# Decoder trunk on one core: where layer 1's output projection starts feed-forward's loads, and who halves one of its weight blocks

## The chip, the core and the metric

The kernel runs on one core of a Trainium2 chip. The metric is the time of one execution in microseconds of the device; the median of three runs before the change is 1432.92 us (1432.63 to 1433.38). All points of time below are microseconds from the first instruction of one profiled execution.

## The reference, cut to what matters

Two layers, each a mixer block and a feed-forward block on 512 tokens of width 1024:

```python
x  = x + g1 * (merged @ w_out)                      # output projection
h2 = rmsnorm(x, norm2_w) * (1 + sc2) + sh2          # second norm
x  = x + g2 * ((silu(h2 @ w_gate) * (h2 @ w_up)) @ w_down)
```

`g1`, `g2`, `sc2`, `sh2` come from `c` through a matrix `w_ada`; everything is float32, with features on the 128 partitions and tokens along the free dimension.

## The kernel before

**A product.** TensorE gets float32 accuracy from three passes (`mm3`, L176): weight-high by data-high, weight-high by data-low, weight-low by data-high. So each weight block of 8 x 128 columns (512 KB) is fetched into a `raw` tile and halved into a `whi` and a `wlo` tile. There are two ways of halving. `split_w` (L515 and L518): ScalarE copies the high half, VectorE subtracts it from `raw`. `split_by_transfer` (L539, L540, L542): ScalarE writes high and minus high, and a transfer issued by POOL adds the block from memory once more onto `wlo`. The pools are small: three `raw` tiles (`RAW = 3`), five `whi`, five `wlo`, six `w` tiles for sums of blocks, 46 `big` tiles.

**Queues.** Fetches leave from SP's queue, transfers that accumulate from POOL's queue; each queue is worked in order, and an issue that waits for its tile holds everything behind it. During layer 1's output projection `in_order[0]` is set: there `sent` pins the transfers of a queue to the order of the program text. VectorE's halvings (L518) are pinned among each other as well; the other instructions of VectorE and ScalarE are placed by a planner that reorders them by its own estimate of when they are ready.

**Layer 1's output projection** (`tail`, L1576, with `middle=out_pairs`, L1646). Of the eight output column blocks, 0 and 1 are plain. Blocks 2 to 5 are the *quad*: two pairs computed with a seven-product scheme from seven weight loads, called S0 to S6 here (`Out.load`, L384). Its products come in this order, each for both pairs (z = 0, 1), each group four `mm3` of 256 columns: B11, B21, R1, -V, B22, T3, T4. S0 and S1 serve B11 and B21, S2 and S3 serve R1 and -V, S4 and S5 serve B22 and T3, S6 alone serves T4. After each group VectorE adds the result to `x` (`put`, L1649); T4 of a pair goes into the same accumulator that T3's `put` has just read. Then `tail` does blocks 6 and 7 (called C6 and C7) in two halves of 256 tokens; in the middle of block 6's second half TensorE sums the squares for the second norm of the first 256 tokens (`lead`, `stat`, the `pair<-big,ones` products). Then come feed-forward's first rows.

**Loads around it.** `next_w` loads up to five blocks ahead. The list after S6 is C6, C7, then R0 to R3 (feed-forward's first rows: gate and up, two blocks of k each, two fetches of 256 KB), then the first `GateUp` pair. That pair needs for each of gate and up a *raw block* (512 KB, `Sums.fetch`), two `w` tiles with fetches from SP and accumulating transfers from POOL (`Sums.begin`, L286, 2 x 256 KB each way), and two additions by VectorE (`Sums.add`, L321 and L322). `opening` (L547) starts gate's part from inside `out_pairs`: "fetch" begins the sums and fetches the raw block, "add" does the two additions. Up's sums are begun by `load_w` when R0 is loaded. Gate's raw block keeps its `raw` tile until the first pair is computed, much later.

**S6** (`Out.load`, sub 6) is halved like this: raw fetched from SP (L393), high and minus high by ScalarE (L394, L395), two accumulating transfers of 256 KB from POOL (L397).

**The dots.** Sixteen dot products with `w_ada` (`ada_halves`, two 128x512 instructions each, L672) give `g1` and `g2` of layer 1. `timed_dots` places them by a list of ticks (`DOT_TICKS`, one tick is 2048 output columns of TensorE); each dot's two fetches of 256 KB into `big` tiles (L668) are placed three ticks before it. Ticks 32 and 33 lie in the attention stage, ticks 46 to 52 in the last gates before the output projection.

Of the kernel before, what the change touches and what calls it, by code (L numbers as in the profile page):

```python
# [13 lines left out]
F32R = mybir.dt.float32r  # L14
BF16 = mybir.dt.bfloat16
I32 = mybir.dt.int32
AF = mybir.ActivationFunctionType
ALU = mybir.AluOpType
# [3 lines left out]
P = 128  # L22
# [19 lines left out]
C_BLOCKS = 8  # L42
# [32 lines left out]

DELAY = 3

DOT_TICKS = (6, 7, 18, 19, 21, 32, 33, 37, 40, 42, 44, 45, 46, 47, 48, 49)

TWO_PI = 2.0 * math.pi  # L80
RED1 = 6.28125
# [16 lines left out]
def hybrid_trunk(ctx, tc, xT, ws, ada, cols, pool_w, qk_w, crow, pos, con, out):  # L98
    nc = tc.nc
    V, A, T = nc.vector, nc.scalar, nc.tensor  # L100
# [3 lines left out]
    wp = ctx.enter_context(tc.tile_pool(name="wp", bufs=4))  # L104
# [6 lines left out]
    def nm(s):  # L111
        uid[0] += 1
        return f"{s}{uid[0]}"

    def bigt(dt=F32R):
        return big.tile([P, S], dt, tag="big", name=nm("big"))
# [4 lines left out]
    def ps_mm():  # L121
        return psum.tile([P, S], F32, tag="mm", name=nm("mm"), bufs=4)

    def ps_pair():
        return psum.tile([P, 2, S], F32, tag="pair", name=nm("pair"), bufs=2)
# [4 lines left out]
    def sm(shape, dt=F32, tag="sm", bufs=8):  # L130
        return small.tile(shape, dt, tag=tag, name=nm(tag), bufs=bufs)

    f32 = lambda ap: ap.bitcast(F32)
# [44 lines left out]
    def pin(ins):  # L178
        return tc.keep_in_program_order(ins)
# [83 lines left out]
    in_order = [False]  # L263

    def sent(ins):
        return pin(ins) if in_order[0] else ins
# [5 lines left out]
    HK = KT // 2  # L272
# [3 lines left out]
    class Sums:  # L276
# [12 lines left out]
        raw = None  # L289
# [38 lines left out]
    class GateUp:  # L328
# [10 lines left out]
        def load(self, sub):  # L339
            if sub < 2:  # L340
                return self.pair[sub].first(self.adding and sub == 0)
            if sub < 6:
                return self.pair[sub % 2].sums(sub // 2 - 1)
            raw = rawt()
            blocks = self.pair[0].blocks(1, 1) + self.pair[1].blocks(1, 1)
            fetch(raw, self.l, blocks)
            return split_w(raw, len(blocks))
# [32 lines left out]
    class Out(GateUp):  # L380
# [3 lines left out]
        def load(self, sub):  # L384
            if sub < 2:
                s = self.pair[sub]
                s.fetch()
                return split_by_transfer(s.raw, self.l, s.column(0))
            if sub < 6:
                return self.pair[sub % 2].sums(sub // 2 - 1)  # L390
            raw, hi, lo = rawt(), *[wp.tile([P, C_BLOCKS, P], F32R, tag=t, name=nm(t), bufs=5) for t in ("whi", "wlo")]
            for z, s in enumerate(self.pair):
                sent(nc.sync.dma_start(raw[:, z * HK:(z + 1) * HK], s.source(1, 1)))  # L393
            A.activation(hi, raw, AF.Copy)  # L394
            A.activation(lo, f32(hi), AF.Copy, scale=-1.0)  # L395
            for z, s in enumerate(self.pair):
                sent(nc.gpsimd.dma_start(lo[:, z * HK:(z + 1) * HK], s.source(1, 1), accum_op=ALU.add))  # L397
            return hi, lo

    class KeyValue:  # L400
        SUBS = 14
# [107 lines left out]
    def rawt():  # L509
        return wp.tile([P, C_BLOCKS, P], F32, tag="raw", name=nm("raw"), bufs=RAW)  # L510

    def split_w(raw, n):
        hi = wp.tile([P, C_BLOCKS, P], F32R, tag="whi", name=nm("whi"), bufs=5)
        with tc.issue_after(hold_hi[0].ins) if hold_hi[0] is not None else nullcontext():
            A.activation(hi[:, :n], raw[:, :n], AF.Copy)  # L515
        lo = wp.tile([P, C_BLOCKS, P], F32R, tag="wlo", name=nm("wlo"), bufs=5)
        with tc.issue_after(hold[0].ins) if hold[0] is not None else nullcontext():
            ins = V.tensor_sub(lo[:, :n], raw[:, :n], f32(hi)[:, :n])  # L518
        pin(ins)
        return hi, lo  # L520
# [13 lines left out]
    def split_by_transfer(raw, l, blocks):  # L534
        n = len(blocks)
        hi = wp.tile([P, C_BLOCKS, P], F32R, tag="whi", name=nm("whi"), bufs=5)
        lo = wp.tile([P, C_BLOCKS, P], F32R, tag="wlo", name=nm("wlo"), bufs=5)
        with tc.issue_after(last_gate[0].ins) if last_gate[0] is not None else nullcontext():
            A.activation(hi[:, :n], raw[:, :n], AF.Copy)  # L539
            A.activation(lo[:, :n], f32(hi)[:, :n], AF.Copy, scale=-1.0)  # L540
        for i, m, src in runs(l, blocks):
            sent(nc.gpsimd.dma_start(lo[:, i:i + m].rearrange("p b n -> p (b n)"), src, accum_op=ALU.add))  # L542
        return hi, lo
# [2 lines left out]

    def opening(z, what):  # L547
        sums = next(s for s, _ in list(items)[at[0]:] if type(s) is GateUp)
        if what == "fetch":
            for s in sums.pair[:1] if in_order[0] else sums.pair:  # L550
                s.begin()
            sums.pair[z].fetch()
        else:
            sums.pair[z].add()
# [7 lines left out]
    def load_w():  # L562
        while at[1] < min(at[0] + 1 + SUMS_AHEAD, len(items)):
            sums, sub = items[at[1]]
            if sums is not None and sub == 0:
                sums.begin()
            at[1] += 1
        sums, what = items[at[0]]
        at[0] += 1
        if sums is not None:  # L570
            return sums.load(what)
        l, blocks = what
        if raws:
            raw = raws.popleft()
        else:
            raw = rawt()
            fetch(raw, l, blocks)
        if by_transfer(l, blocks):
            return split_by_transfer(raw, l, blocks)
        with tc.issue_after(split_after[0].ins) if split_after[0] is not None else nullcontext():  # L580
            halves = split_w(raw, len(blocks))
        if (l, blocks[0]) == (0, ("in", 0, 3)):
            rotary()
        return halves
# [29 lines left out]
    def next_w(ahead=None):  # L614
        ahead = ahead_now[0] if ahead is None else ahead
        while at[0] < len(items) and len(loaded) <= ahead:
            loaded.append(load_w())
        return loaded.popleft()
# [59 lines left out]
    def timed_dots(l):  # L678
# [3 lines left out]
        def load(i):  # L682
            fetched[i] = ada_halves(l, BESIDE[l][i // KT], i % KT, False)

        for i, at_tick in enumerate(DOT_TICKS):
            events.append((at_tick - DELAY, 0, lambda i=i: load(i)))
# [419 lines left out]
    sums = scratch[:, 0].rearrange("p (t n) -> p t n", n=P)  # L1106
# [36 lines left out]
    y, t, r = [sm([P, TT], tag="rst", bufs=3) for _ in range(3)]  # L1143
# [22 lines left out]
    for l in range(L):  # L1166
# [7 lines left out]
        for n, (k, lo, hi) in enumerate([(k, 0, S) for k in range(KT)] if l == 0 else HALVES + REST):  # L1174
# [19 lines left out]
            w = held[k]  # L1194
# [191 lines left out]
        for j in range(2):  # L1386
# [12 lines left out]
            z = bigt(F32)  # L1399
# [133 lines left out]
        for step, j in GATE2:  # L1533
# [13 lines left out]
            t = sg2.pop(j)  # L1547
# [97 lines left out]
        def out_pairs():  # L1645

            def put(n, src, c):
                by = (minus if n % 2 else mod[l][:, G1])[:, n:n + 1]
                return V.scalar_tensor_tensor(x[n][:, c], src, by, x[n][:, c], op0=ALU.mult, op1=ALU.add)  # L1649

            both, fm = range(2), out_forms
            n1, n2_ = OUT_FIRST, [n + 1 for n in OUT_FIRST]
            a, c = [None] * 2, [None] * 2
            w = [next_w() for _ in both]
            for z in both:
                a[z] = ps_mm()[:, :BLOCK]
                group(a[z], w[z], 0, "B11", True, fm, True)
                put(n1[z], a[z], early)
            e = ps_pair()
            for z in both:  # L1660
                group(e[:, z, :BLOCK], w[z], 1, "B21", True, fm, True)
            for z in both:
                ins = put(n1[z], e[:, z, :BLOCK], early)
            with tc.issue_after(ins.ins):
                for i in range(HK):
                    out_form_two(i)
            w = [next_w() for _ in both]
            for z in both:
                c[z] = ps_mm()[:, :BLOCK]
                group(c[z], w[z], 0, "R1", True, fm)  # L1670
                put(n2_[z], c[z], late)
            for z in both:
                group(a[z], w[z], 1, "-V", False, fm)
                put(n1[z], a[z], late)
            opening(0, "fetch")
            w = [next_w() for _ in both]
            for z in both:
                group(c[z], w[z], 0, "B22", False, fm)
                put(n1[z], c[z], late)
                n2.add(n1[z], 0, S)  # L1680
            for z in both:
                group(a[z], w[z], 1, "T3", False, fm)
                put(n2_[z], a[z], late)
            opening(0, "add")
            w = next_w()
            for z in both:
                group(a[z], w, z, "T4", False, fm)
                put(n2_[z], a[z], early)
                n2.add(n2_[z], 0, S)

        ahead_now[0] = 4
        if l == 0:
# [359 lines left out]
```

## Time and profile before

| | us |
|---|---|
| median of three runs | 1432.92 |
| the profiled execution, whole | 1433.26 |
| its span, first to last instruction | 1431.5 |
| TensorE busy in the span | 1420.0 |
| VectorE busy | 1102.9 |
| ScalarE busy | 779.7 |
| POOL busy | 146.6 |

The span is 1.76 us shorter than the profiled execution, which is 0.34 us above the median. TensorE's own loads of weights overlap its products. In the rows, PE is TensorE, DVE is VectorE, ACT is ScalarE, SPq is SP's queue; `mm` and `pair` are accumulators, `x` the residual stream, `in_ws` the weights in memory.

### The profile page before, as it was taken

How to read it: one execution, taken by the hardware profiler on the slowest of the kernel's cores; microseconds unless marked ns; L12 is line 12 of the kernel's file. 1: busy time of each engine (PE TensorE's matmuls, PEld its weight loads, DVE VectorE, ACT ScalarE, POOL GpSimd, SP SyncE). 2: the span in 40 equal slices, each digit the busy share in tenths (PEclk: the TensorE clock that was granted, in tenths of full speed). 3: DMA queues.
4: the chain of work that ended last, by engine and by line, in shares of the span. 5: the costliest groups of instructions: out<-in, count | busy, mean ns of one | idle time of the engine just before them, and what ended most of it. 6: DMA issues, size and time to landing. Idle time of an engine off the chain costs nothing.

```text
span 1431.5 us, 23124 instructions
## 1 busy us (share of the span) xinstructions
PE 1420.0 (99%) x8600; PEld 1265.8 (88%) x8600; DVE 1102.9 (77%) x2097; ACT 779.7 (54%) x1317; POOL 146.6 (10%) x181
## 2 busy tenths in 40 slices
PE   9999999999999999999999999999999999999998
PEld 8888888888998998999988888878888989989998
DVE  8989888768897867776799986766878847657676
ACT  6667667633762542545455775665557625435452
POOL 0111001101010201010002001010210101000110
PEclk9999999999999999999999999999999999999999
DMA  9757788867366767655447566678964637636452
GB/s 384 229 141 208 207 218 209 234 203 222 92 164 209 208 171 208 185 164 181 168 161 215 172 172 160 161 190 219 255 147 111 175 112 185 171 107 185 135 129 82
DMA packets 114449, 259.35 MB, mean 181 GB/s; under 512 B 13208, under 2 KB 33824, under 8 KB 114336
## 3 DMA queue, kind: packets, MB, share of 16 engines
q1 hardware_dynamic: 87616, 198.22, 40.6%
q0 software_dynamic: 26128, 59.52, 23.6%
q8 instruction: 67, 1.10, 0.3%
q14 instruction: 46, 0.38, 0.1%
q10 hardware_dynamic: 592, 0.14, 0.0%
HBM read 255.73 MB, written 2.10 MB: 180 GB/s over the span
## 4 chain that ended last, share of the span: by engine, by line
PE 97%; DVE 1%; DMA 1%; ACT 0%; issue 0%; SPq 0%; POOL 0%; ACTq 0%; DVEq 0%; POOLq 0%
PE mm L176 81%; PE pair L176 14%; PE mm L182 2%; DMA raw<-in_ws 1%; DVE big L860 0%; DVE wlo L518 0%; ACT whi L515 0%; DVE big L1549 0%; DVE big L1501 0%; DVE w L377 0%; DVE w L378 0%; ACT whi L539 0%; DVE w L639 0%; ACT big L845 0%; DVE big L863 0%
## 5 line engine op out<-in xcount | busy, mean ns | idle before, releaser
L176 PE MATMUL mm<-big,whi 128*128 128x256 f32 (+1 forms) x4442 | 1066.6, 333 | 1.6 <-DVE x L1649 1.5
L176 PEld LDWEIGHTS mm<-big,whi 128*128 128x128 f32 x4442 | 752.7, 191 | 79.4 <-issue 2.6
L176 PE MATMUL mm<-big,wlo 128*128 128x256 f32 (+1 forms) x2221 | 736.3, 332 | 0.0
L176 PEld LDWEIGHTS mm<-big,wlo 128*128 128x128 f32 x2221 | 422.9, 190 | 40.3 <-issue 0.3
L515 ACT ACTIVATE whi<-raw 128x1024 fp32r<-128x1024 f32 (+2 forms) x174 | 181.5, 1047 | 158.7 <-PE mm L176 81.5
L518 DVE TENSOR_TENSOR wlo<-raw,whi 128x1024 fp32r<-128x1024 f32 (+2 forms) x174 | 208.0, 1203 | 45.6 <-ACT whi L515 45.3
L515 ACT ACTIVATE whi<-w 128x1024 fp32r<-128x1024 f32 (+1 forms) x100 | 104.7, 1049 | 165.8 <-PE mm L176 94.9
L518 DVE TENSOR_TENSOR wlo<-w,whi 128x1024 fp32r<-128x1024 f32 (+1 forms) x100 | 119.2, 1209 | 27.6 <-ACT whi L515 26.8
L286 POOL DMA_DIRECT2D w<-in_ws x86 | 75.1, 964 | 542.3 <-DMA w<-in_ws 218.2
L542 POOL DMA_DIRECT2D wlo<-in_ws x53 | 45.5, 859 | 464.5 <-ACT wlo L540 310.7
L176 PE MATMUL pair<-big,whi 128*128 128x256 f32 (+1 forms) x476 | 91.7, 290 | 0.0
L1566 DVE SCALAR_TENSOR_TENSOR x<-mm,mod,x 128x512 f32<-128x512 f32 (+1 forms) x76 | 52.2, 690 | 46.9 <-PE mm L176 46.5
L639 DVE SCALAR_TENSOR_TENSOR w<-w,csil 128x1024 f32<-128x1024 f32 x64 | 76.6, 1219 | 13.2 <-DMA w<-in_ada 13.2
L176 PE MATMUL pair<-whi,big 128*128 128x512 f32 x256 | 82.3, 389 | 0.0
L176 PEld LDWEIGHTS pair<-big,whi 128*128 128x128 f32 x476 | 75.8, 192 | 1.9
L539 ACT ACTIVATE whi<-raw 128x1024 fp32r<-128x1024 f32 x53 | 56.3, 1062 | 26.5 <-PE mm L176 18.3
L176 PE MATMUL pair<-big,wlo 128*128 128x256 f32 (+1 forms) x238 | 69.0, 290 | 0.0
L176 PEld LDWEIGHTS pair<-whi,big 128*128 128x128 f32 x256 | 48.1, 188 | 9.8
L540 ACT ACTIVATE wlo<-whi 128x1024 fp32r<-128x1024 f32 x53 | 56.1, 1058 | 0.7
L859 ACT ACTIVATE big<-big 128x512 fp32r<-128x512 f32 x56 | 34.5, 624 | 30.1 <-DVE big L1238 14.7
L176 PE MATMUL pair<-wlo,big 128*128 128x512 f32 x128 | 49.2, 389 | 0.0
L860 DVE TENSOR_TENSOR big<-big,big 128x512 fp32r<-128x512 f32 x56 | 38.4, 687 | 11.2 <-ACT big L859 10.9
(253 smaller groups left out, 1484.3 us busy)
## 6 DMA issues: line engine op xcount, KB each, us to landing
raw<-in_ws SPq DMA_DIRECT2D x144, 512.0 KB, 4.2
w<-in_ada SPq DMA_DIRECT2D x64, 512.0 KB, 5.8
wlo<-in_ws POOLq DMA_DIRECT2D x53, 512.0 KB, 7.4
raw<-in_ws SPq DMA_DIRECT2D x86, 256.0 KB, 4.1
w<-in_ws SPq DMA_DIRECT2D x84, 256.0 KB, 3.2
w<-in_ws POOLq DMA_DIRECT2D x84, 256.0 KB, 6.0
big<-in_ada SPq DMA_DIRECT2D x64, 256.0 KB, 5.1
raw<-in_ws SPq DMA_DIRECT2D x16, 448.0 KB, 5.2
```

Source lines behind the costliest of these rows:

```text
L176: tc.keep_in_program_order(T.matmul(*a, **k))
L182: tc.keep_in_program_order(T.transpose(*a))
L286: sent(queue.dma_start(dst[:, i * P:(i + n) * P], src, **how))
L515: A.activation(hi[:, :n], raw[:, :n], AF.Copy)
L518: ins = V.tensor_sub(lo[:, :n], raw[:, :n], f32(hi)[:, :n])
L539: A.activation(hi[:, :n], raw[:, :n], AF.Copy)
L540: A.activation(lo[:, :n], f32(hi)[:, :n], AF.Copy, scale=-1.0)
L542: sent(nc.gpsimd.dma_start(lo[:, i:i + m].rearrange("p b n -> p (b n)"), src, accum_op=ALU.add))
L639: return V.scalar_tensor_tensor(aw, aw, 1.0, csil, op0=ALU.mult, op1=ALU.mult, accum_out=mod[l][:, part, j:j + 1])
L859: last_copy[0] = A.activation(hi, src, AF.Copy)
L860: last_split[0] = V.tensor_sub(lo, src, f32(hi))
L1566: V.scalar_tensor_tensor(x[k][:, lo:hi], src, mod[l][:, part, k:k + 1], x[k][:, lo:hi], op0=ALU.mult, op1=ALU.add)
```

## The change

Four edits, all in layer 1:

- S6 is halved by `split_w`: the minus-high copy of ScalarE and the two transfers of POOL are gone, a subtraction by VectorE is new.
- Gate's sums are begun at the start of `out_pairs` (a new "begin" of `opening`), ahead of S6's fetch in program order.
- "fetch" (gate's raw block) stands behind the two loads that follow -V, which are those of C7 and R0, instead of ahead of them; it now begins both sums, of which gate's have been begun at the start and up's by the load of R0. "add" stands behind T4 instead of ahead of it, and so behind the load of R1.
- The dots of ticks 32 and 33 are gone from the list, ticks 50 and 51 are new: `g1` is complete at tick 42 instead of 37, `g2` at 51 instead of 49.

```diff
-DOT_TICKS = (6, 7, 18, 19, 21, 32, 33, 37, 40, 42, 44, 45, 46, 47, 48, 49)
+DOT_TICKS = (6, 7, 18, 19, 21, 37, 40, 42, 44, 45, 46, 47, 48, 49, 50, 51)
@@ Out.load, sub 6
-            raw, hi, lo = rawt(), *[wp.tile([P, C_BLOCKS, P], F32R, tag=t, name=nm(t), bufs=5) for t in ("whi", "wlo")]
+            raw = rawt()
             for z, s in enumerate(self.pair):
                 sent(nc.sync.dma_start(raw[:, z * HK:(z + 1) * HK], s.source(1, 1)))
-            A.activation(hi, raw, AF.Copy)
-            A.activation(lo, f32(hi), AF.Copy, scale=-1.0)
-            for z, s in enumerate(self.pair):
-                sent(nc.gpsimd.dma_start(lo[:, z * HK:(z + 1) * HK], s.source(1, 1), accum_op=ALU.add))
-            return hi, lo
+            return split_w(raw, 2 * HK)
@@ opening
-        if what == "fetch":
-            for s in sums.pair[:1] if in_order[0] else sums.pair:
+        if what == "begin":
+            sums.pair[z].begin()
+        elif what == "fetch":
+            for s in sums.pair:
                 s.begin()
             sums.pair[z].fetch()
@@ out_pairs
+            opening(0, "begin")
             ...
             for z in both:
                 group(a[z], w[z], 1, "-V", False, fm)
                 put(n1[z], a[z], late)
+            w = [next_w() for _ in both]
             opening(0, "fetch")
-            w = [next_w() for _ in both]
             ...
-            opening(0, "add")
             w = next_w()
             for z in both:
                 group(a[z], w, z, "T4", False, fm)
                 put(n2_[z], a[z], early)
                 n2.add(n2_[z], 0, S)
+            opening(0, "add")
```

## Rows read from the trace of the kernel before

**Rows 1.** Busy times of the page: busy us, share, instructions.
```profile
PE 1420.0 (99%) x8600; PEld 1265.8 (88%) x8600; DVE 1102.9 (77%) x2097; ACT 779.7 (54%) x1317; POOL 146.6 (10%) x181
```
**Rows 2.** Waits of PE, whole span: us in total, times, longest.
```profile
PE pair L176 <- ACT big L792: 3.8, 1, 3.8
PE mm L176 <- DVE x L1649: 1.5, 1, 1.5
```
**Rows 3.** Busy by stretch: length, PE, PEld, DVE, ACT, POOL, PEclk, DMA share, GB/s.
```profile
1061.55:1063.24 1.69, 0.15 (x2) 0.00 (x1) 1.64 (x3) 0.00 (x0) 0.00 (x0) 1.00 1.06 256
1063.24:1071.98 8.74, 8.74 (x72) 8.69 (x72) 4.47 (x8) 1.88 (x3) 0.00 (x0) 1.00 0.96 248
1071.98:1075.50 3.52, 0.16 (x2) 0.00 (x0) 2.21 (x4) 1.60 (x4) 0.00 (x0) 1.00 0.01 3
...
1077.66:1084.07 6.41, 6.41 (x37) 6.41 (x37) 4.58 (x11) 4.30 (x10) 0.00 (x0) 0.63 0.30 100
```
**Rows 4.** Chain of work that ended last, 1052 to 1078: start, us, what.
```profile
1052.98 1.07 ACT whi L539
...
1054.44 5.32 DMA raw<-in_ws
...
1062.59 8.98 DMA raw<-in_ws
...
1077.28 0.58 PE pair L176
```
**Rows 5.** Timeline of SP's queue, 1028 to 1076: start, us, issues merged.
```profile
1032.48 17.65 SPq L270 DMA_DIRECT2D raw<-in_ws  x2
```
**Rows 6.** Issues at 1049.8 and at 1057.7: count, KB each, median us to landing.
```profile
raw<-in_ws SPq DMA_DIRECT2D x1, 512.0 KB, 4.0
...
raw<-in_ws SPq DMA_DIRECT2D x2, 256.0 KB, 7.2
```
**Rows 7.** Timeline of POOL, 1010 to 1106.
```profile
1012.85 0.87 POOL L542 DMA_DIRECT2D wlo<-in_ws  x1 [2.98 <-ACT wlo L540]
...
1051.16 2.43 POOL L397 DMA_DIRECT2D wlo<-in_ws  x2 [21.44 <-ACT wlo L395]
1055.80 0.86 POOL L542 DMA_DIRECT2D wlo<-in_ws  x1 [2.22 <-ACT wlo L540]
1056.35 3.86 POOL L286 DMA_DIRECT2D w<-in_ws  x4
```
**Rows 8.** Busy by stretch (columns of Rows 3) ahead of and in the crowded stretch.
```profile
1036.00:1052.00 16.00, 15.91 (x107) 14.40 (x106) 14.54 (x28) 10.68 (x16) 0.84 (x2) 1.00 0.18 63
1052.00:1072.00 20.00, 18.46 (x153) 18.19 (x152) 13.56 (x24) 8.01 (x11) 5.99 (x7) 1.00 1.04 244
```
**Rows 9.** Timeline of DVE, 1047 to 1064: start, us, line, operation, [idle before <-releaser].
```profile
1056.49 1.22 DVE L518 TENSOR_TENSOR wlo<-raw,whi 128x1024 fp32r<-128x1024 f32 x1
...
1060.96 1.23 DVE L518 TENSOR_TENSOR wlo<-raw,whi 128x1024 fp32r<-128x1024 f32 x1 [1.62 <-ACT whi L515]
...
1062.71 0.48 DVE L1649 SCALAR_TENSOR_TENSOR x<-mm,c,x 128x256 f32<-128x256 f32 x1
```
**Rows 10.** Timeline of ACT, 1030 to 1106: high halves of S6 and R1.
```profile
1048.71 1.06 ACT L394 ACTIVATE whi<-raw 128x1024 fp32r<-128x1024 f32 x1 [0.43 <-PE pair L176]
...
1066.22 1.06 ACT L515 ACTIVATE whi<-raw 128x1024 fp32r<-128x1024 f32 x1 [4.77 <-DMA raw<-in_ws]
```
**Rows 11.** The dots' line, 940 to 1020: count, ns min/median/max, first and last start.
```profile
L672 DVE SCALAR_TENSOR_TENSOR big<-big,csil x22: 679/684/692, 948.6 to 1012.7; 128x512 f32<-128x512 f32 x22
```
**Rows 12.** Timeline of DVE behind the last dot, 1009 to 1037.
```profile
1018.15 0.69 DVE L1501 SCALAR_TENSOR_TENSOR big<-big,mm 128x512 f32<-128x512 f32 x1 [3.26 <-PE mm L176]
```
**Rows 13.** Waits of SP's queue, 940 to 1000: us in total, times, longest.
```profile
SPq L668 <- DVE big L672: 18.7, 7, 6.3
```
**Rows 14.** Timeline of DVE: the low halves of the first rows' first and sixth k.
```profile
1081.73 0.48 DVE L830 SCALAR_TENSOR_TENSOR big<-tmp,mod,big 128x256 fp32r<-128x256 f32 x1 [0.40 <-ACT big L825]
...
1089.72 0.48 DVE L830 SCALAR_TENSOR_TENSOR big<-tmp,mod,big 128x256 fp32r<-128x256 f32 x1
```

## The prediction

> **What bounds the kernel now.** I read the busy times first: TensorE is busy 1420.0 of 1431.5 us [rows 1], so time can be won only where it waits or runs slowly. The second view, TensorE's waits, names two places of size, and both lie in the stretch that the change edits: 1.5 us behind a `put` of VectorE and 3.8 us behind the squares for the second norm [rows 2]. The third view gives the price of that stretch [rows 3]. A product (three matmuls of 256 columns) takes 8.74 / 24 = 0.364 us at full clock. TensorE does next to nothing from 1061.55 to 1063.24 (1.69 us lost), stops again at 1071.98 and has the norm's four `ones` products done at 1077.86 [rows 3, 4]; these are worth some 0.48 us, so 5.4 us are lost. In the pause the clock stays at 1.00 until 1075.50; from 1077.66 to 1084.07 its mean is 0.63, because part of the stretch runs at 1.2 GHz, and the 12 products there take 6.41 us instead of 12 x 0.364 = 4.37: 2.04 us more. Together 9.1 us, 0.64%: the most that this edit can win.
>
> Why TensorE waits is read from the chain of waits: it leaves TensorE and runs through fetches [rows 4]. R0 leaves when C6's high half is made (1054.05) and lands 5.32 us later; R2 leaves when R0's low half is made and takes 8.98 us. R2's high half stands in ScalarE's queue ahead of the squares that the norm needs. A 512 KB block took 4.0 us with the queues nearly empty, R1 7.2 us in the crowd [rows 6]. The crowd: the transfer engines are used 0.18 of the time from 1036 to 1052, and fully (1.04, 244 GB/s) from 1052 to 1072 [rows 8]. There POOL's queue holds S6's two transfers, C6's one and four of the first sums, all behind S6 at 1051.16 [rows 7]; SP's queue stood still before that, since C7's fetch waited behind gate's raw block for S6's tile until 1049.80 [rows 5].
>
> **The change, part by part.** *Gate's raw block moved back, S6 halved by VectorE, gate's sums begun early.* In units of 512 KB, these leave or land after 1049.8 now: C7, up's sums (SP), S6's two, C6, gate's sums, up's sums (POOL), R0, R1, R2: nine. After: C7 takes the tile that gate's raw block held and leaves near 1032.5; up's two fetches follow it in the idle stretch; gate's sums leave before S6, both ways; S6's two transfers are gone; gate's raw block comes in behind R0. R0, gate raw, R1, R2, C6 and up's sums remain: six. Three units fewer are 3 x 0.524 MB / 244 GB/s = 6.4 us of the crowd. On POOL's queue four transfers of 256 KB are gone ahead of C6's and up's; on SP's queue R1 and R2 now have gate raw ahead of them.
>
> R0's tile is now free when VectorE has made S6's low half, not when ScalarE has read it. S6's high half ends at 1049.77 [rows 10]; a low half takes 1.22 us [rows 9]. VectorE's first gap for it I put at 1051.7 to 52.9 (estimate); the bounds are 1050 and 1057.7, with C7's low half pinned behind it. R0 then leaves at 1052.9 and lands after 4.0 to 5.3 us, at 1057 to 58.3. From there the buffers of high halves rule: R0's waits for T3 of z = 0, which ends two groups (2 x 1.46 us) ahead of 1061.55, at 1058.65. High half 1.06 us, low half from 59.8; today it starts at 1060.96, behind 1.62 us of idling, and the `put` for which TensorE waits starts 1.75 us behind it, at 1062.71 [rows 9]. So: `put` 61.55 to 62.05, T4 of z = 1 at 62.1 instead of 63.24, **1.1 us won** (bounds 0 and 1.69). The new 1.22 us of VectorE lie in that 1.62 us of idling; with that cover gone they would cost up to 1.2 us here. ScalarE's 1.06 us saved are beside other work.
>
> R1 and R2: how the two queues share is read from R2, whose 512 KB took from R1's landing (its high half starts on it at 1066.22 [rows 10]) to 1062.59 + 8.98 = 1071.57 [rows 4]: 5.4 us, 97 GB/s of 244, while POOL's queue was full. With that half for SP as long as POOL has work, and some 290 GB/s alone (estimate: 512 KB in 4.0 us less 2.2 us of leaving and landing): R0 and most of gate raw go before C6's transfer of 1055.8, the rest of gate raw to 58.5, R1 to 63.6, POOL's two units end at 64.1, R2 lands at 66.7 (bounds 65.2, from 244 GB/s shared by all six, and 71.6 as now). From R2's landing to the end of the norm's products it is 1077.86 - 1071.57 = 6.3 us today [rows 4]; gate's two additions now lie in that run on VectorE (L321, L322, about 1.2 us, half of it beside other work): 0.6 us more. End at 1073.6 instead of 1077.86: **4.3 us won, the 1.1 among them** (bounds 0 and 7.1).
>
> A page bears on this sharing. The Trainium skill (DMA: Bandwidth & Descriptors, section Queues, rings and completion order) says that each transfer engine takes turns among the queues that have work, a packet at a time; that speaks against the change, since bytes taken from POOL's queue help SP's only once POOL's runs empty, while gate raw is added to SP's. R2's 97 GB/s sides with it. With turns the sum is the one here; with the pooled rate it would be 1.5 us less.
>
> *The clock.* TensorE now comes to the norm's products at 1071.98 - 1.1 = 1070.9 and has them at 1073.6, so it pauses 2.2 us. The pause of 1.69 us left the clock alone, and of the long one the first 3.52 us were still at 1.00 [rows 3]. So I take no fall: **2.05 us won**.
>
> *What is late next.* Today the first k of the first rows has its low half at 1082.21, 4.35 us behind the norm's products, and the sixth at 1090.20 [rows 14]; TensorE wants them at 1084.07 and at 1084.07 + 20 x 0.364 + 0.48 = 1091.8. At full clock TensorE needs 4.37 us from the products to the rows, so the slack of 1.6 to 1.9 us shrinks by 2.05: **0.75 us given back** (bounds 0 and 1.9).
>
> *Begin, add and the wait of SP.* SP and POOL now have gate's fetches and transfers ahead of S6 and C6; S6 is wanted first at 1060.1 and C6 behind it, and they hold up SP only if their `w` tiles are taken. Up's fetches come ahead of R0 as before. "Add" moved behind T4 no longer stands ahead of T4's `put`s; it waits for gate raw (about 1060) and so for nothing.
>
> *The two late dots.* 4 x 0.68 us of VectorE [rows 11] move from the attention stage to the end of the gates, where VectorE is idle for 3.26 us ahead of 1018.15 [rows 12]; cost nothing there, at most 2.7 us if that cover is missed. Their four fetches of 256 KB come later on SP's queue.
>
> Sum: 4.3 + 2.05 - 0.75 = 5.6 us. The profiled execution is 1433.26 us, its span 1431.5, the median of the runs 1432.92; against the median, **1427.3 us**.
>
> **The rivals.** *The clock falls all the same.* A pause between 1.69 and 3.52 us is not in the trace. Then the 2.05 us stay lost and nothing is given back: 1432.92 - 4.3 = 1428.6; with the longer pause that would go with it, about 1429.2. The Trainium skill (TensorE: Matmul & The Clock Gate, Part 1) says that the watch on activity runs freely and does not start with a pause, so the same length can go either way; its rule would give this rival. Chance 0.17.
>
> *S6's low half comes late.* If the planner places it at its bound, 1056.5 to 57.7, R0 leaves at 57.7 into the crowd, 3.7 us later than now, with gate raw, R1 and R2 behind it on SP: R0 lands near 62, its `put` near 65.4 (2.2 us lost at T4), and R2 at 69.5 to 70.3, the norm near 1077: 0 to 1 us won. With half of that delay, up to 2.8. 1430.1 to 1432.9, say 1431.5. For it: VectorE is busy 14.5 of 16 us up to 1052 [rows 8]. Against: the low half is ready to go at 1049.8. Chance 0.20; this is also the case in which the edit doesn't do what it says.
>
> *SP held by the late dots.* Today the dots' fetches wait 18.7 us in all for `big` tiles that earlier dots free [rows 13]. If the fetches of ticks 50 and 51 meet a full pool, they hold back blocks 0, 1, S0 and S1 behind them. Block 0 has time to spare: its transfer leaves at 1012.85 [rows 7], R2's 8.98 us bounds its landing [rows 4], and TensorE starts on it near 1031 (the quad's 13 groups of 1.46 us and two plain blocks of 16 x 0.364 us ahead of 1061.55), so 9 us. Beyond that each us goes on the path; from 9 + 5.6 + 2.9 = 17.5 us on the change is slower. At 20 us: 1432.92 + 11 - 5.6 = 1438.3. Against: the longest of those waits is 6.3 us, and attention's own tiles come free before. With other ways to lose, chance 0.13.
>
> **How the numbers follow.** About 0.2% (2.9 us) is what a measurement of this kernel can tell from no change. Forecast 0.50 (1424.8 to 1429.2, from the norm's end at 1072.0 to 1075.5 and 0 to 1.9 us given back), fallen clock 0.17, late low half 0.20, slower 0.13. Faster by over 0.2%: 0.67; within: 0.20; slower: 0.13. The range 1424.8 to 1432.2 holds nearly all of the first two and most of the third.
>
> **What would show it.** Right: R2 lands before 1068, no wait of TensorE over 1 us at T4, a pause before the norm's products under 3 us and a granted clock of 1.00 behind it, transfer engines busy from 1032 to 1042, L518 of S6 near 1052. Wrong: S6's low half behind 1055; R1 or R2 still over 7 us; a stretch at half clock near 1075; SP's L668 waiting behind 1000; a new wait of TensorE for a low half of C6 (its transfer leaves at 1055.8 [rows 7], wanted at 1062.1 + 1.46 = 1063.6) or of the first rows.

## The result

The change made the kernel slower: 1443.43 us against 1432.86 us, the ratio 1.0073 with a 95% interval of 1.0059 to 1.0087. The forecast was 1427.3 us, and the range did not hold the time. One run each of this kernel, e7 and e8 took 2339.25, 1536.98 and 1737.31 us at mean granted clocks of 0.556, 0.851 and 0.752: the medians given here count it, the ratios don't, and without it the medians are 1442.97, 1427.06 and 1431.81 us. The profiled execution has a span of 1441.2 us, 9.7 us more than before.

The waits of TensorE in the kernel after, whole span (us in total, times, longest), answer to [rows 2]:

```profile
PE mm L176 <- ACT big L857: 5.7, 2, 4.4
PE pair L176 <- ACT big L790: 3.4, 1, 3.4
PE mm L176 <- DVE tmp L1769: 1.6, 1, 1.6
PE mm L176 <- DMA wlo<-in_ws: 1.4, 1, 1.4
...
PE mm L176 <- DVE x L1647: 0.6, 1, 0.6
```

The wait that the change was meant to shorten at T4 did shrink, from 1.5 to 0.6 us. The pause for the norm's squares (L790, which was L792) is 3.4 us instead of 3.8. What is new is larger: 5.7 us for high halves of `merged` (L857), the data that the output projection multiplies, so ahead of everything that three of the four edits touch. Busy times by stretch (columns of [rows 3]):

```profile
1033.70:1038.08 4.38, 0.00 (x0) 0.03 (x1) 4.34 (x10) 4.13 (x6) 1.38 (x4) 0.81 1.08 250
1036.50:1043.30 6.80, 5.22 (x12) 4.13 (x13) 6.80 (x13) 3.19 (x5) 2.63 (x3) 0.50 1.08 220
...
1045.08:1046.42 1.34, 0.00 (x0) 0.00 (x0) 0.65 (x3) 0.66 (x2) 0.00 (x0) 1.00 1.13 226
...
1083.15:1086.50 3.35, 0.00 (x0) 0.00 (x0) 3.26 (x7) 0.88 (x3) 0.00 (x0) 1.00 0.06 22
1087.60:1091.00 3.40, 3.17 (x15) 3.17 (x16) 1.93 (x5) 0.68 (x2) 0.00 (x0) 0.50 0.66 227
```

TensorE stands still for 4.38 us and again for 1.34 us; from 1036.50 on the granted clock is 0.50 (the 1.2 GHz level) for 6.8 us, of which 5.2 us lie behind the stop and cost half of that, 2.6 us. With the transient of 1.6 us in layer 0 (L1769, in no other profile here) and small stops that are 0.3 us longer in all than before, this is 10.2 us. It agrees with a second count: the wait ahead of T4 begins at 1072.03 instead of 1061.7, 10.3 us later, and from there to the end of the span the kernel after needs 1441.2 - 1072.03 = 369.2 us against 1431.5 - 1061.7 = 369.8. So the whole loss is made ahead of T4, and the edits of the projection together are worth 0.6 us in this execution.

Where it comes from is seen in SP's queue. First its waits of the kernel after, 985 to 1050, then its timeline (start, us, issues merged), then the timeline of the kernel before for the same stretch:

```profile
SPq L666 <- DVE big L670: 16.5, 6, 6.8
...
SPq L666 <- DVE big L1547: 7.9, 1, 7.9
```
```profile
999.27 11.29 SPq L666 DMA_DIRECT2D big<-in_ada  x4
1010.62 2.63 SPq L367 DMA_DIRECT2D w<-in_ws  x4
1013.35 12.43 SPq L270 DMA_DIRECT2D raw<-in_ws  x6
```
```profile
996.45 3.10 SPq L367 DMA_DIRECT2D w<-in_ws  x4
999.64 15.61 SPq L270 DMA_DIRECT2D raw<-in_ws  x6
```

The four fetches of the last two dots (L666, was L668) wait 7.9 us for a `big` tile that the attention stage frees, and then for tiles of earlier dots. The sums of the quad and the next weight blocks stand behind them in SP's queue. The sums leave 14.2 us later (1010.62 instead of 996.45), the blocks 13.7 us (1013.35 instead of 999.64). Down the line, on VectorE (start, us, line, operation, [idle before <-releaser]):

```profile
1020.61 1.22 DVE L514 TENSOR_TENSOR wlo<-raw,whi 128x1024 fp32r<-128x1024 f32 x1 [7.80 <-ACT whi L511]
...
1033.13 0.69 DVE L858 TENSOR_TENSOR big<-big,big 128x512 fp32r<-128x512 f32 x1 [3.34 <-ACT big L857]
```

The low half of the attention block fetched at 1013.35 is made at 1020.61 (at 1010.91 before), and VectorE idles 7.8 us for it. The chain of waits of the kernel after (start, us, what) goes on from there through the next late block:

```profile
1021.86 6.50 DMA raw<-in_ws
1028.39 1.07 ACT whi L535
...
1032.58 0.53 ACT big L857
...
1033.13 0.69 DVE big L858
```

Its high half (L535) and what is queued behind it on ScalarE hold the high half of `merged` (L857) until 1032.48, and VectorE's next work waits another 3.34 us for that; TensorE stops at 1033.70.

### The profile page after: what moved, and what is told of

Same layout as the page of the kernel before. It is cut to its first block, busy times and chain, and to the rows that moved or that the text cites. A ratio compares the mean times of both kernels' runs of the same rounds, so it can differ in the third digit from the quotient of the medians.

```text
span 1441.2 us, 23127 instructions
## 1 busy us (share of the span) xinstructions
PE 1421.8 (99%) x8600; PEld 1265.8 (88%) x8600; DVE 1104.1 (77%) x2098; ACT 779.2 (54%) x1316; POOL 144.1 (10%) x179
## 4 chain that ended last, share of the span: by engine, by line
PE 82%; issue 9%; DVE 4%; DMA 3%; ACT 1%; SPq 0%; POOL 0%; ACTq 0%; DVEq 0%; POOLq 0%
PE mm L176 69%; PE pair L176 11%; DMA raw<-in_ws 2%; PE mm L182 2%; DVE wlo L514 1%; DMA w<-in_ws 1%; DVE big L858 0%; ACT whi L511 0%; DMA x<-in_xT 0%; DVE big L1547 0%; DVE x L1647 0%; ACT big L857 0%; DVE w L438 0%; DVE big L670 0%; DVE big L1499 0%
## 5 line engine op out<-in xcount | busy, mean ns | idle before, releaser
L637 DVE SCALAR_TENSOR_TENSOR w<-w,csil 128x1024 f32<-128x1024 f32 x64 | 76.6, 1219 | 14.3 <-DMA w<-in_ada 14.2
L535 ACT ACTIVATE whi<-raw 128x1024 fp32r<-128x1024 f32 x53 | 56.3, 1062 | 21.7 <-PE mm L176 14.9
L857 ACT ACTIVATE big<-big 128x512 fp32r<-128x512 f32 x56 | 34.3, 624 | 36.8 <-DVE big L1547 17.7
```

Source lines behind the costliest of these rows:

```text
L637: return V.scalar_tensor_tensor(aw, aw, 1.0, csil, op0=ALU.mult, op1=ALU.mult, accum_out=mod[l][:, part, j:j + 1])
L857: last_copy[0] = A.activation(hi, src, AF.Copy)
```

## The experiments

### Which edit loses the time

**e1_ticks_old**: the change without its fourth edit.

```diff
-DOT_TICKS = (6, 7, 18, 19, 21, 37, 40, 42, 44, 45, 46, 47, 48, 49, 50, 51)
+DOT_TICKS = (6, 7, 18, 19, 21, 32, 33, 37, 40, 42, 44, 45, 46, 47, 48, 49)
```

> The change with the old list of ticks (dots at 32 and 33 again, none at 50 and 51); the other three edits stay. Theory A (the late dots' fetches hold SP's queue for a `big` tile, and that is the whole loss): TensorE's waits at 1033 and 1045 are gone, the time falls by 8 to 14 us to 1430 to 1434. Whether the 5.6 us forecast for the other edits come with it is open: after them C6's transfer landed 1.4 us too late and R2 landed only 1.5 us earlier relative to the quad, so I expect little, 1431 to 1433. Rival B (the loss is in the edits of the projection itself): it stays above 1440.

Measured 1433.97 us, ratio to before 1.0008 [0.9999, 1.0017]. The loss is gone, but nothing is won: the three edits of the projection are worth nothing together.

**e2_ticks_only**: the kernel before with the new ticks alone (the same line, the other way round).

> The kernel before with the new list of ticks alone. Theory A: the same wait of SP of 8 us near 1000 to 1008, TensorE waiting 4 to 6 us for merged's high halves and some 3 us at half clock; 1441 to 1445. Rival B: 1432 to 1434, since only 2.7 us of VectorE's work move into a stretch where it is idle.

Measured 1443.19 us, 1.0069 [1.0055, 1.0082]. The ticks alone make the whole loss.

**e3_late_on_pool**: the change, with the fetches of the last two dots issued from POOL's queue.

```diff
-    def ada_halves(l, part, j, later=True):
+    def ada_halves(l, part, j, later=True, queue=None):
         ...
-            nc.sync.dma_start(tiles[h], ada[l, part, j][:, h * S:(h + 1) * S])
+            (queue or nc.sync).dma_start(tiles[h], ada[l, part, j][:, h * S:(h + 1) * S])
         ...
-            fetched[i] = ada_halves(l, BESIDE[l][i // KT], i % KT, False)
+            fetched[i] = ada_halves(l, BESIDE[l][i // KT], i % KT, False, nc.gpsimd if i >= 14 else None)
```

> The change, with the fetches of the last two dots (ticks 50 and 51) issued from POOL's queue in place of SP's; they wait for the same `big` tiles, but hold POOL's queue. Theory A (what costs is that SP stands): attention's weight blocks and the quad's sums leave SP near 997 again; 1431 to 1436. Rival C (what costs is the dots' own work and their late data on VectorE, pinned ahead of the halvings): VectorE still waits for them, 1440 to 1445.

Measured 1436.85 us, 1.0022 [1.0014, 1.0031], with runs from 1433.53 to 1438.42: some two thirds of the loss come back. The waits moved along with the fetches, as POOL's waits from 985 to 1060 show (us in total, times, longest):

```profile
POOL big L666 <- DVE big L1547: 9.9, 1, 9.9
POOL big L666 <- DVE big L670: 9.0, 1, 9.0
```

**e8_late_no_fetch**: the change, with the last two dots computed on the tiles of the dot before them, so that their four fetches don't exist. This leaves out the data of two columns of `g2`.

```diff
-        def dot():
+        def dot(j=j):
         ...
-            fetched[i] = ada_halves(l, BESIDE[l][i // KT], i % KT, False)
+            fetched[i] = ada_halves(l, BESIDE[l][i // KT], i % KT, False) if i < 14 else None
+            if i == 13:
+                reused.append(fetched[i])
-            events.append((at_tick, 1, lambda i=i: fetched.pop(i)()))
+            events.append((at_tick, 1, lambda i=i: (fetched.pop(i) or reused[0])(i % KT)))
```

> The change with the new ticks, but the two last dots (ticks 50 and 51) fetch nothing and compute on the tiles of the dot before them, so two columns of g2 are wrong and four fetches of 256 KB are left out. The theory that SP's queue is held by these fetches: SP goes on as with the old ticks, 1434 to 1435.5 us (as the first experiment, 1433.97). The rival, that 2.7 us of VectorE at the end of the gates make the loss (merged's halves and the attention blocks' low halves come late): 1439 to 1443. The run with these fetches on POOL gave 1436.85; if that rest of 2.9 us was POOL's own queue being held, it is gone here, and if it was VectorE's work it stays.

Measured 1431.96 us, 0.9993 [0.9984, 1.0002]. VectorE still has the late dots' arithmetic, and the loss is gone entirely. So the late fetches lose the time, not the 2.7 us of VectorE, and by e3 most of it is lost where they stand at the head of SP's queue. The 2.9 us by which e3 lies above e1 go too. In e3 it is POOL that is held: the quad's sums leave it at 1009.10, here at 1003.88. Whether the fetches' own bytes have a share in the 2.9 us was not tried, nor why e8 lies 0.15% under e1. SP's timeline is that of before again:

```profile
998.93 16.05 SPq L270 DMA_DIRECT2D raw<-in_ws  x6
```

### Why the projection's edits won nothing

**e4_s6_only**: the kernel before with S6 halved by `split_w`, nothing else.

```diff
-            A.activation(hi, raw, AF.Copy)
-            A.activation(lo, f32(hi), AF.Copy, scale=-1.0)
-            for z, s in enumerate(self.pair):
-                sent(nc.gpsimd.dma_start(lo[:, z * HK:(z + 1) * HK], s.source(1, 1), accum_op=ALU.add))
-            return hi, lo
+            return split_w(raw, 2 * HK)
```

> The kernel before with one edit: S6 halved by ScalarE and VectorE, its two transfers of POOL gone. By the forecast's reckoning (one unit of 512 KB less in the crowd, 2.1 us, and R0's tile free when VectorE is done) R2 lands 1 to 2 us earlier and the norm's products come 1 to 2 us earlier: 1430.5 to 1432. If the low half comes late (as in the trace of the change, 1.8 us ahead of C7's), R0 leaves later and nothing is won: 1432.5 to 1434.

Measured 1434.37 us, 1.0007 [0.9998, 1.0016]. Nothing is won: T4 no longer waits, but the pause ahead of the norm grew to 5.5 us and the clock falls behind it.

The stretch is therefore read in the trace of e1. Its waits of TensorE from 1050 to 1100, its chain of waits (start, us, what), and its busy times in the norm's pause and behind it:

```profile
PE pair L176 <- ACT big L790: 3.3, 1, 3.3
PE mm L176 <- DMA wlo<-in_ws: 1.1, 1, 1.1
PE mm L176 <- DVE x L1647: 0.6, 1, 0.6
```
```profile
1062.50 8.21 DMA raw<-in_ws
...
1070.81 1.06 ACT whi L511
...
1073.03 0.68 DVE w L321
...
1074.03 0.68 DVE w L322
...
1076.21 0.43 ACT big L790
```
```profile
1073.35:1076.68 3.33, 0.00 (x1) 0.00 (x0) 3.24 (x7) 0.88 (x3) 0.00 (x0) 0.86 0.03 12
1076.68:1083.10 6.42, 6.35 (x29) 5.89 (x29) 4.45 (x11) 2.95 (x7) 0.00 (x0) 0.54 0.51 163
```

T4 waits 0.6 us, and R2 lands at 1070.71, 0.9 us earlier than before. Both gains are spent at once: 1.1 us on a new wait for C6's transfer, and 1.36 us on gate's two additions (L321, L322), which now stand between R2's high half and the squares. The pause is 3.33 us, the clock falls behind it. From this came two suspects. Theory A: the additions, put behind T4 in the text, are pinned behind R1's low half, and this waits for R1. Theory B: the transfers in the crowd set the end by themselves.

**e5_add_back**: e1 with the additions ahead of the load that precedes T4 again.

```diff
+            opening(0, "add")
             w = next_w()
             for z in both:
                 group(a[z], w, z, "T4", False, fm)
                 ...
-            opening(0, "add")
```

> The kernel of the first experiment (the change with the old ticks), with gate's two additions ahead of the load that precedes T4 again. Why the projection's edits won nothing in the first experiment, theory A: the additions are pinned behind R1's low half, which waits for R1 (landed 1068.3); so they run at 1073.0 to 1074.7, between R2's high half and the squares of the norm, and eat the 0.9 us by which R2 landed earlier. Then they go back into VectorE's idle stretch of 6.0 us ahead of 1069.5, the squares come some 1.2 us earlier, the pause shrinks from 3.33 to about 2.1 us: 1432.8 us, and 1430.8 if the clock does not fall behind the shorter pause. Theory B, the transfers alone set the norm's end (R2's landing 1070.7): no change, 1434.0 within 0.7.

Measured 1431.92 us, 0.9991 [0.9982, 1.0]; against e1's 1.0008 that is 0.17%, 2.4 us. Theory A holds for this part. The first addition, in the timeline of VectorE, now runs where VectorE idled in e1:

```profile
1062.72 0.68 DVE L321 TENSOR_TENSOR w<-w,raw 128x512 f32<-128x512 f32 x1
```

The pause is 1.74 us. But the clock falls behind it all the same, for 3.4 us:

```profile
1072.74:1074.48 1.74, 0.01 (x2) 0.00 (x1) 1.65 (x4) 0.47 (x2) 0.00 (x0) 1.00 0.02 7
1076.90:1080.30 3.40, 3.40 (x18) 3.40 (x18) 3.30 (x9) 2.43 (x5) 0.00 (x0) 0.51 0.25 96
```

**e7_c6_vector**: e1 with C6 halved by VectorE as well, the additions where the change has them.

```diff
-OUT_APART = (0, 1, 6)
+OUT_APART = (0, 1)
```

> The kernel of the first experiment, with C6 halved by VectorE instead of by a transfer: 512 KB leave the crowd, and up's two transfers on POOL no longer stand behind C6's of 1057.6 and can go near 1041, when their targets have landed. Theory B: R1 lands 2 to 4 us earlier, R2 3 to 4 us earlier (near 1067), TensorE's wait of 1.1 us for C6's transfer is gone, the norm's products end about 3 us earlier: 1430 to 1431 us, 1428.5 to 1429 if the clock stays. Theory A: R1's low half comes earlier too, so the additions come ahead of R2's high half of their own accord and cost nothing any more; the same gain, so this run is read by its trace. Against both: VectorE gets 1.22 us more of work near 1056 to 1061 where it is 2.8 to 3.0 of 3.0 us busy; if C6's or C7's low half or R0's comes late, T4 and block 6 wait by up to 1.2 us and nothing is won: 1433 to 1435.

Measured 1427.77 us, 0.9960 [0.9946, 0.9974]. Theory B holds, and it is the larger part. POOL's last transfers ahead of the crowd leave at 1041.65 and 1043.29; in the crowd it has none. The share of the queues, first in e1 (1054 to 1076), then here (1054 to 1072): packets, MB, share of the 16 engines' time:

```profile
q1 hardware_dynamic: 1152, 2.62, 37.3%
q0 software_dynamic: 432, 1.05, 27.9%
```
```profile
q1 hardware_dynamic: 1232, 2.79, 49.8%
```

In e1 a MB of POOL's accumulating transfers (q0) takes 27.9 / 1.05 = 26.6% of that stretch, a MB of SP's fetches (q1) 37.3 / 2.62 = 14.2%: 1.9 times as much, with packets of about the same mean size. The same is seen where both queues work at once: from 1059 to 1068 in e1, 1.03 MB of POOL take 67.0% of the engines' time and 1.08 MB of SP 37.4%. It is the accumulating that costs and not POOL's queue, as far as e3 shows: there two plain fetches from POOL (0.52 MB, 11.8% of 996.9 to 1008) take 22.7% per MB, SP's beside them (3.28 MB, 85.8%) 26.2%. Without POOL's transfers in the crowd R1 and R2 take 3.6 and 3.8 us (median of their two fetches), against 8.2 each in e1. The fetch on the chain is R1 here (below), in e1 it was R2. TensorE's one wait left from 1060 to 1100 is 0.4 us:

```profile
1059.87 3.73 DMA raw<-in_ws
```
```profile
PE pair L176 <- DVE big L786: 0.4, 1, 0.4
```

**e6_add_back_c6_vector**: both edits on top of e1.

> Both of the edits above. If the additions and the crowd are two separate causes, the gains add up to no more than the better of the two plus 1 us, since both end at the squares: 1428.5 to 1431. If VectorE is full ahead of T4 (C6's low half and two additions are 2.5 us more there), TensorE waits at T4 for over 1 us: 1433 to 1435.

Measured 1426.71 us, 0.9957 [0.9945, 0.997]: 6.3 us under the kernel before. It can't be told from e7, as expected, since both edits end at the squares. R2 lands at 1067.37. The pause and what follows:

```profile
1071.28:1071.75 0.47, 0.00 (x1) 0.00 (x0) 0.38 (x2) 0.47 (x2) 0.00 (x0) 1.00 0.00 0
1073.07:1080.00 6.93, 6.93 (x57) 6.93 (x58) 5.83 (x15) 5.02 (x11) 0.00 (x0) 1.00 0.30 108
```

T4's 1.5 us are gone, the pause is 0.5 + 0.4 us instead of 3.8, and the clock stays at 1.00, worth 2.0: 1.5 + 2.9 + 2.0 = 6.4 us, against 6.3 measured.

### Which edits the gain needs

**e9_before_c6_vector**: the kernel before with C6 halved by VectorE alone (the diff of e7).

> The kernel before, with one edit: C6 halved by VectorE. Does it need the change's edits to win? Theory 1 (the three raw tiles): before, R0 takes C6's raw tile when ScalarE has read it (1054.05); now it must wait for C6's low half by VectorE, near 1057.7, so R0 leaves 3.5 us later, TensorE waits 2 to 3 us at T4, and the bytes saved are lost again: 1432 to 1435 us. Theory 2 (the crowd alone): one unit of 512 KB less and no 1.2 us pause behind it: R2 lands some 2 us earlier, 1430 to 1431 us.

Measured 1433.18 us, 0.9994 [0.9985, 1.0002]: nothing. R0 now waits for C6's low half, as theory 1 has it:

```profile
1057.43 1.23 DVE wlo L518
...
1058.71 0.33 SPq L270
...
1059.09 8.35 DMA raw<-in_ws
```

R0 leaves at 1058.71, 4.6 us later than before. The place of the loss was not as expected: TensorE doesn't wait at T4, and the pause ahead of the norm is 4.9 us.

**e10_s6_transfers**: e6 with S6 halved by transfers again (the diff of e4 backwards).

> The kernel of the seventh experiment (additions ahead of T4, C6 by VectorE, 1426.7 us), with S6 halved by transfers again, as before. S6's two transfers come onto POOL at 1051, ahead of the crowd; VectorE has 1.22 us less, and R0 can leave when ScalarE has read S6 (near 1051) instead of at 1057.1. If VectorE's halving of S6 is what the gain needs: 1430 us or more. If raw tiles and POOL's free queue carry it and S6's edit is worth nothing: 1425.5 to 1427.5 us, R0 lands near 1056, no wait over 0.5 us at T4.

Measured 1427.35 us, 0.9951 [0.9939, 0.9962]: as good as e6. With the raw block behind R0, S6's edit is not needed. POOL has as many transfers in the crowd here as in e1 (S6's two and up's two, 1.05 MB). But R0 leaves at 1050.08 instead of 1054.94, and POOL's transfers leave from 1051.44 on instead of 1057.62: they have moved their last byte when R2 leaves at 1061.53, and R2 takes 3.9 us. So POOL's queue has to be done by the time of R2; it need not be empty. T4 waits 0.6 us, a little over the 0.5 expected.

**e11_raw_back**: e6 with gate's raw block ahead of the loads of C7 and R0 again.

```diff
+            opening(0, "fetch")
             w = [next_w() for _ in both]
-            opening(0, "fetch")
```

> The kernel of the seventh experiment (1426.7 us), with gate's raw block fetched ahead of C7 and R0 again, as before. It then holds one of three raw tiles from 1033 on, so C7 waits for S6's low half (near 1057) and R0 for C6's (near 1058) and R1 for C7's or R0's. If the raw tiles set when the rows' loads leave: T4 or block 6 waits 2 to 4 us, 1429.5 to 1433 us. If only bytes in the crowd count (gate raw leaves it): 1425 to 1426.5 us.

Measured 1428.88 us, 0.9963 [0.9951, 0.9975]. The interval overlaps that of e6; the medians, each against its own runs of before, differ by 6.3 - 4.4 = 1.9 us. The trace has the cost: the pause is 0.90 us, and the clock is at 0.50 for 3.40 us behind it.

```profile
1070.92:1071.82 0.90, 0.00 (x1) 0.00 (x1) 0.81 (x4) 0.47 (x2) 0.00 (x0) 1.00 0.99 401
1073.90:1077.30 3.40, 3.40 (x18) 3.40 (x18) 2.86 (x7) 2.00 (x5) 0.00 (x0) 0.50 0.46 171
```

The expected wait at T4 or in block 6 is not there. Most of the gain stays, although the raw block stands where it stood in e9. What e11 has and e9 lacks is S6's edit, the early beginning of gate's sums and, since "fetch" now begins both sums, up's sums ahead of C7's load: their fetches leave SP at 1034.76 instead of 1052.44. The three bring 4.3 us here. POOL's transfers for the sums are all issued by 1044.57 in e11; in e9 four of them begin at 1054.90, behind S6's. So C6's edit needs company: either these three, or the raw block moved with one of the other two edits (e10, e12). Which of the three counts in e11 was not tried.

**e12_no_early_begin**: e6 without the line `opening(0, "begin")`.

> The kernel of the seventh experiment (1426.7 us), without the early beginning of gate's sums: they begin with gate's raw block, behind R0, so two fetches and two transfers of 256 KB come into the stretch from 1057 on. By the crowd's bytes (1 MB more at some 250 GB/s, shared with R0, gate raw, R1 and R2), R2 lands 2 to 4 us later and the additions, which wait for the transfers, come behind R1's low half: 1429 to 1431.5 us. If the early beginning is worth nothing: 1426.7 within 0.7.

Measured 1426.90 us, 0.9948 [0.9936, 0.996]: the early beginning is worth nothing here. The text order lets the sums begin with the raw block, but SP issues their fetches at 1032.87 all the same, well ahead of the crowd, and POOL their transfers from 1038.09 on: once no transfer of S6 and C6 stands ahead of them in POOL's queue, they leave when their targets have landed.

## Why the prediction was wrong, point by point

**The late dots** were costed at nothing, and this is the step that failed. The price of VectorE's part was right (e8), the DMAs of the step were not followed to what stands behind them in SP's queue. The rival "SP held by the late dots" names the mechanism that happened, and its chance of 0.13 was too low for two reasons. Its slack was taken from block 0 (9 us); the first to suffer were the attention's own blocks and the quad's sums. With the hold of 13.7 us its rule gives 1432.92 + 4.7 - 5.6 = 1432.0 us, and 1443.4 was measured. And "attention's own tiles come free before" was argued without a row: the 7.9 us are a wait for just such a tile (L1547). [Rows 13] showed that these fetches meet a full pool; moved to later ticks they meet it later, where less slack is left behind them.

**R0 and T4**: 1.1 us were forecast; the wait shrank to 0.62 us in e1 (forecast about 0.55), a win of 0.9. The reason given was wrong in part. S6's low half came at 1056.08, at its late bound, so the second rival's condition held; but R0 did not wait for it, since it took C6's tile, which ScalarE had read by 1054.92. So this rival's price at T4 was not paid.

**R2 at 1066.7** was the mis-sized term, 4.0 us early (1070.71 in e1, whose stretch runs 0.8 us later than before). The rate and the sharing came out: from 1059 to 1068 in e1 the queues move 235 GB/s (forecast 244), and 1.08 of 2.11 MB are SP's (forecast: half). Wrong was when the work begins and ends. The crowd began at 1054.9 instead of 1052.9, and up to R2's landing the engines work only some 0.79 of the time, where the forecast took them as full (busy by stretch, columns of [rows 3]):

```profile
1055.00:1071.00 16.00, 14.29 (x117) 13.91 (x117) 9.84 (x16) 6.20 (x9) 2.63 (x3) 1.00 0.79 198
```

POOL's two units (C6's, up's sums) were to end at 64.1; they left from 1057.62 on, 1.8 us later than before, and worked until 1068. For R2 they are the larger weight: at 1.9 times the time per byte they stand for almost four of SP's units. This price was not read, though the queue table of the page before has it (packets, MB, share; about 4 of POOL's 59.52 MB are plain by the program's text):

```profile
q1 hardware_dynamic: 87616, 198.22, 40.6%
q0 software_dynamic: 26128, 59.52, 23.6%
```

That is 0.40% per MB of POOL's against 0.20% of SP's, again the factor 1.9. From 1059 to 1068 in e1 POOL's queue moves 414 packets and SP's 491. The Trainium skill (DMA: Bandwidth & Descriptors, section Queues, rings and completion order) has the engines take turns by packets; these counts side with it, and what a packet costs in time was the part that was missing. For the 2.2 us of leaving and landing behind the forecast's 290 GB/s no row was given; what the runs show of SP alone is R1 and R2 of e7, 3.6 and 3.8 us.

**The additions** were put at 0.6 us in the norm's run; they took 1.36. The pin behind R1's low half was in the text of the change ("and so behind the load of R1") and its consequence, that they wait for R1's landing, was not drawn.

**C6's transfer** (1057.62 instead of 1055.80) was 8.4 us on the way and cost 1.1 us. The prediction lists this among its signs of error, and gives it no price.

**The clock**: "no fall" rested on one pause of 1.69 us and on the first 3.52 us of the long one, behind which the clock did fall [rows 3]. In e1 the pause is 3.33 us, so the first rival's condition (a fall) held by way of R2; in e5 a pause of 1.74 us brings a fall as well. So the first rival was the right one on the clock even where the pause was short.

**Given back**: 0.75 us were taken off for the first rows. In e6, the case that the forecast describes, TensorE is busy 6.93 of 6.93 us behind the norm at full clock: nothing is given back. The forecast's own slack of 1.6 to 1.9 us against 2.05 would have given 0.2 to 0.4 us.

**Two slips in the sums** decide nothing: six units at 244 GB/s from 1052.9 end at 65.8, not 65.2, and the forecast's slow end with 1.9 us given back is 1430.4, not 1429.2.

The forecast's time is reached (1427.3 us forecast, 1426.7 measured in e6), but by another kernel and with other terms: C6's transfer is gone, the additions are ahead of T4 and the old ticks stay, and 1.5 + 2.9 + 2.0 us stand where 1.1 + 3.2 + 2.05 - 0.75 were forecast. That the two numbers are so near is in part luck. Not tried were e6 without the early beginning and with S6 by transfers at once, and e6 with the new ticks.

## What to carry to other kernels

An issue in a queue costs what stands behind it: when a step moves, follow each of its fetches to the tile it waits for and to the first block behind it with little slack, not to the block that comes to mind. Transfers that accumulate are to be weighed in engine time from the queue table, not in bytes, and placed by when they are done. And a saving in a chain of waits is worth nothing until the next item in line, here an addition pinned behind a late load and the clock behind the pause, is moved as well.

## What the runs showed of the hardware

An accumulating transfer from POOL's queue takes 1.9 times the time of the transfer engines that a plain fetch from SP's queue takes for the same bytes: 26.6% against 14.2% per MB in the crowded stretch of e1. Over the whole span of the kernel before the two queues, about 4 MB of POOL's being plain, have the same factor. Two plain fetches from POOL's queue (e3) took no more than SP's, 22.7% against 26.2% per MB.

The length of a pause does not tell whether the clock falls: it stayed at 1.00 behind the 1.54 us of T4 in the kernel before, and fell for 3.4 us behind 0.90 us (e11) and 1.74 us (e5), and for 3.4 us behind 3.35 us (the kernel after, 1087.60 to 1091.00); behind 3.33 us in e1 its mean over 6.42 us is 0.54. The Trainium skill (TensorE: Matmul & The Clock Gate, Part 1) calls the watch on activity free-running, so a pause does not start it; the traces agree with that as far as they go.
